# A two-block transformer step with 64 experts on one core: modulation's last sums taken in later, the transposed norm split between two engines, one head more between scores and transposes

## The chip, the cores and the metric

The kernel runs on one core of one Trainium2 chip. The metric is the device time of one execution in microseconds (us). Engines: PE (TensorE, matmuls; its weight loads are PEld), DVE (VectorE), ACT (ScalarE), POOL (GpSimd) and SP (SyncE, which issues nearly all loads). Each engine works through its own list of instructions in order; they meet at semaphores. Nothing is scheduled by hardware across engines, so the order in which the program issues work is the order in which an engine does it.

## What is computed

256 tokens of width 1024 go through two blocks. The first has a gated spatial branch and differential attention, ends in a layer norm, and shares the input projections. The second takes its scales, shifts and gates from a condition vector `c` (modulation), has two attentions (one with forget gates) and a mixture of 64 experts of which each token uses 6. All in fp32.

```python
def second_block(x, c, ...):
    cond = jax.nn.silu(c)
    for l in range(DEPTH):                                  # DEPTH is 1
        mod = cond @ w_mod[l] + b_mod[l]                    # 1024 x 6144
        shift_m, scale_m, gate_m, shift_f, scale_f, gate_f = ...split(mod, N_MOD)
        h = rms_norm_2(x, g_mix_norm[l]) * (1.0 + scale_m) + shift_m
        x = x + gate_m * hybrid_mixer(h, ...)
        h = rms_norm_2(x, g_ffn_norm[l]) * (1.0 + scale_f) + shift_f
        x = x + gate_f * moe_ffn(h, ...)
    return rms_norm_2(x, g_final)

# in hybrid_mixer
log_f = jax.nn.log_sigmoid((f_logit + b_forget).astype(jnp.float32))
cum_log_f = jnp.cumsum(log_f, axis=1).transpose(0, 2, 1)
o_fox = causal_block_attention(heads(fq), heads(fk), heads(fv), ..., cum_log_f)

# in the first block
lam = exp(sum(b_lam_q1 * b_lam_k1)) - exp(sum(b_lam_q2 * b_lam_k2)) + lam_init
x = layer_norm(DEEPNORM_ALPHA * x + mix_out + ple, ln_g[i], ln_b[i])
```

## The kernel before

**Dense stages (0 to about 600 us).** A matmul in fp32 is done as three: the weight is split into a rounded part (`hi`) and the rest (`lo`), the activations likewise, and hi by hi, lo by hi and hi by lo are summed. Weights come in slabs of 1 MB through SP's queue into 22 slots of 8 KB per partition. ACT casts a 512-column piece to `hi` (line 209), DVE subtracts it to give `lo` (line 210). `unit` (line 244 issues its matmuls where tokens are the moving side, line 242 the other way) runs one slab against 128 or 256 tokens, and calls `beat` after each group of three matmuls. `beat` is what orders the program: it advances the generators registered as streams (`yield n` means "go on n beats later"), then splits one more piece of a coming slab, or does one "extra", which is one sum of the modulation. `finish` runs a generator to its end at once. While `hold` is set, no extras are taken. Matmuls accumulate in three to five PSUM banks; the others (`bank()`) are handed out in turn.

**Early.** `early` makes the rope tables and SiLU of `c` with ACT's Sigmoid (line 765) and a POOL product; `prep_lam` (line 800) makes lambda with ACT's Exp (line 805). Each function needs a table of its own, loaded by an ACT_TABLE_LOAD. The rope of the first projections is DVE's `m` (lines 725 to 727), which reads an accumulation bank and so frees it.

**Modulation.** `w_mod` comes in 24 slabs, 8 for each of three blocks of two vectors. DVE adds each slab's products into `mod_acc` (line 580). `mod_finish` sums the 128 partitions by matmuls with ones (line 523), copies the sums (ACT, line 525), writes them to DRAM as `mod_line` (line 527, ACT's DMA queue), reads them back spread over partitions (line 538 for columns, 512 KB at line 535 for a gate), and adds the bias (DVE, lines 547 and 544). `mod_ready(blk)` forces the outstanding sums and then finishes the block's generator at once. For the last block that happens just ahead of the stage that multiplies by `w_out` (line 1395); `scale_f` (line 1414) follows.

**Norms.** `enter2(t)` does, for one half of the tokens, the layer norm that ends block 1, the rms norm `xn` (line 1119) and `scaled_T`: 8 transposes on PE (line 341), four to a bank, scaled and shifted by ACT into `hi` (lines 350, 354) and again by DVE into `val` (lines 352, 356), from which DVE subtracts `hi` (line 357).

**Attention of block 2.** `forget` makes `logf` on DVE and ACT (lines 1222 to 1229) and cumulates it with small matmuls (lines 1232 to 1234); DVE writes the result into a column of `lat_fq` and `fk` (lines 1237, 1238), which `heads_T` transposes (line 1274). `soft_heads` runs 16 heads in all, three steps of a head spread by `skewed`: `scores` (line 1284 on PE, maxima on DVE, Exp on ACT, division on DVE, line 1297), `transposed` (line 1305), `weighted` (line 1316):

```python
return b.skewed(range(8), (scores, transposed, weighted), 1)
```

While step i of the loop issues the scores of head i, it issues the transposes of head i-1 and the products of head i-2.

**Experts (about 612 to 1051 us).** 192 MB of expert weights come through SP. The first six experts' loads are issued as soon as slots are free, the others after the routing is known.

Of the kernel before, what the change touches and what calls it, by code (L numbers as in the profile page):

```python
# [68 lines left out]
class Builder:  # L69
# [54 lines left out]
    def tmp(self, shape, dtype, tag):  # L124
        size = 1
        for n in shape[1:]:
            size *= n
        kind, bufs = ("tiny", 12) if size <= 16 else ("small", 6) if size <= 64 else ("medium", 3) if size <= 128 else ("large", 4) if size <= 512 else ("huge", 2)
        if self.fixed:
            kind, bufs = tag, self.fixed.get(tag, 2)  # L130
        return self.work.tile(shape, dtype, tag=kind, name=self.name(tag), bufs=bufs)
# [124 lines left out]
    def beat(self):  # L256
# [11 lines left out]
        if self.quiet:  # L268
            return
        if self.hold or not (self.extras and (self.beats % 3 == 0 or not self.pieces) and self.extras[0][0](self.extras[0][1])):  # L270
# [26 lines left out]
    def skewed(items, stages, gap):  # L297

        n = len(items)
        for i in range(n + len(stages) - 1):  # L300
            for s, stage in enumerate(stages):
                if 0 <= i - s < n:
                    stage(items[i - s])
                yield gap
# [29 lines left out]
    def scaled_T(self, src, t, hi, lo, kts, scale, shift=None):  # L334

        nc = self.nc
        for k in range(0, kts, 4):
# [4 lines left out]
            val = self.tmp([P, n, P], F32, "val")  # L342
            h = hi[:, k:k + n, t * P:(t + 1) * P]
            l = lo[:, k:k + n, t * P:(t + 1) * P]
            for on_act in (True, False):
                for j in range(n):
                    i = ps[:, j * P:(j + 1) * P]
                    sc = scale[:, k + j:k + j + 1]
                    if shift is None and on_act:
                        nc.scalar.activation(h[:, j], i, AF.Copy, scale=sc)  # L350
                    elif shift is None:
                        nc.vector.tensor_scalar(val[:, j], i, sc, None, op0=OP.mult)
                    elif on_act:
                        nc.scalar.activation(h[:, j], i, AF.Identity, scale=sc, bias=shift[:, k + j:k + j + 1])
                    else:
                        nc.vector.tensor_scalar(val[:, j], i, sc, shift[:, k + j:k + j + 1], op0=OP.mult, op1=OP.add)
            nc.vector.tensor_tensor(l, val, h.bitcast(F32), op=OP.subtract)
            yield
# [3 lines left out]
def tile_block(ctx: ExitStack, tc: tile.TileContext, a: dict, out: bass.AP, taps=None):  # L362
# [154 lines left out]
    def mod_finish(blk):  # L517
# [10 lines left out]
        yield 8  # L528
# [10 lines left out]
        yield 8  # L539
# [13 lines left out]
    def mod_ready(blk):  # L553
        while len(mod_streams) <= blk:
            b.run_extra()
        for m in mod_streams[:blk + 1]:
# [203 lines left out]
    b.stream(rest_of_x(), 1)  # L760
    def early():
        tables(pos_i, freq, cos_t, sin_t)
        yield 14
        c_sig = b.tmp([P, KT], F32, "c_sig")
        nc.scalar.activation(c_sig, c_col, AF.Sigmoid)
        nc.gpsimd.tensor_tensor(c_col, c_col, c_sig, op=OP.mult)
# [30 lines left out]

    neg_lam = b.dense([P, 1], F32, "neg_lam")

    def prep_lam():  # L800
        pr = b.tmp([P, 2, 64], F32, "lam_pr")
        nc.vector.tensor_tensor(pr, lam_in[:, 0::2], lam_in[:, 1::2], op=OP.mult)
        sm = b.tmp([P, 2], F32, "lam_sm")
        nc.vector.tensor_reduce(sm, pr, axis=AX.X, op=OP.add)
        nc.scalar.activation(sm, sm, AF.Exp)
        nc.vector.tensor_tensor(neg_lam, sm[:, 1:2], sm[:, 0:1], op=OP.subtract)
        nc.vector.tensor_scalar(neg_lam, neg_lam, -LAM_INIT, None, op0=OP.add)
        yield

    s_lam = b.stream(prep_lam(), 20)  # L810
# [34 lines left out]
    b.finish(s_lam)  # L845
# [373 lines left out]
    def forget():  # L1219
# [10 lines left out]
        yield 6  # L1230
# [17 lines left out]
    g_fk.run((1,))  # L1248
    b.finish(s_lat)
# [28 lines left out]
    def soft_heads(qT, kT, width, v, which):  # L1278
# [43 lines left out]
        return b.skewed(range(8), (scores, transposed, weighted), 1)  # L1322
# [19 lines left out]
    g_fv.run()  # L1342
# [52 lines left out]
    mod_ready(2)  # L1395
# [587 lines left out]
```

## Time and profile before

| what | value |
|---|---|
| time, three runs | 1067.29, 1070.34, 1070.19 us; median 1070.19 |
| the profiled execution | 1065.67 us, of which the span from first to last instruction is 1064.0 |
| mean granted clock of TensorE | 0.963 |
| busy: PE, DVE, ACT, POOL | 968.5 (91%), 562.7 (53%), 412.0 (39%), 28.1 us (3%) |
| moved by DMA | 320.61 MB, 301 GB/s over the span |
| chain that ended last | PE 49%, DMA 32%, DVE 12%, ACT 3% |

How the rows further down are read. A row of the waits: the engine, tile and line that waited, "<-" and whom for, us in total, how often, the longest. A row of the timeline: start in us, length in us, engine, line, operation, output tile "<-" input tiles, shapes, how many in a row ("x4"), and in brackets the idle time of the engine just before it with what ended it. A row of the windows: the stretch in us and its length, then for PE, PEld, DVE, ACT and POOL the busy us and the number of instructions, then TensorE's granted clock as a share of full speed (1.00 is 2.4 GHz, 0.50 is 1.2 GHz), the share of the 16 DMA engines' time that was busy, and GB/s.

### The profile page before, as it was taken

Reading aid. Unit: us, or ns where it says so; the run is one execution under the profiler, and the core shown is the slowest. Engines: PE = TensorE matmul, PEld = TensorE weight load, DVE = VectorE, ACT = ScalarE, POOL = GpSimd, SP = SyncE. Lnnn points to the kernel's source line nnn. Section 1 sums busy time; section 2 is a strip of 40 time slices with the busy share of each in tenths; the row PEclk is TensorE's granted clock in tenths of the full one; section 3 lists DMA queues with packets and bytes.
Section 4 is the critical chain, followed back from the end, with each engine's and each line's share of the span. In section 5 each row is a group of like instructions: output and inputs, shape, how many; then the busy total and the mean of one; then the engine's idle time right before and its main releaser. Section 6 shows DMA issues by size and latency. Waiting matters only on the chain.

```text
span 1064.0 us, 17522 instructions
## 1 busy us (share of the span) xinstructions
PE 968.5 (91%) x6844; PEld 729.7 (69%) x6844; DVE 562.7 (53%) x1204; ACT 412.0 (39%) x897; POOL 28.1 (3%) x89
## 2 busy tenths in 40 slices
PE   8899999999998789898969989999978997699786
PEld 7789889899976677797947656766635664356432
DVE  6886777798879764757747433123322321022112
ACT  5565666554454454454624232121211221122102
POOL 0000000100000010000000100000000000000000
PEclk9999999999999898999989999999989998899988
DMA  8976249485984253253975799999999999999995
GB/s 270 334 268 230 98 144 339 142 307 205 367 290 158 79 206 121 80 198 127 376 319 197 299 417 384 421 422 421 420 420 421 420 421 420 421 420 421 421 415 212
DMA packets 83455, 320.61 MB, mean 301 GB/s; under 512 B 10013, under 2 KB 12317, under 8 KB 56362
## 3 DMA queue, kind: packets, MB, share of 16 engines
q1 hardware_dynamic: 82482, 318.37, 76.9%
q8 instruction: 55, 0.90, 0.3%
q10 hardware_dynamic: 888, 1.09, 0.3%
q14 instruction: 30, 0.25, 0.1%
HBM read 318.37 MB, written 1.07 MB: 300 GB/s over the span
## 4 chain that ended last, share of the span: by engine, by line
PE 49%; DMA 32%; DVE 12%; ACT 3%; issue 2%; SPq 0%; POOL 0%; ACTq 0%; DVEq 0%; POOLq 0%
PE bank L242 15%; PE bank L244 14%; DMA eu<-in_w_exp_up_dram 12%; DMA ed<-in_w_exp_down_dram 8%; DMA eg<-in_w_exp_gate_dram 7%; PE bank L1811 6%; DVE lo L210 5%; PE bank L1720 3%; PE bank L1664 2%; PE bank L1739 2%; DVE mod_acc L580 1%; DMA raw<-in_w_in_dram 1%; DMA mod_acc<-mod_line 1%; PE bank L1536 1%; PE bank L1274 1%
## 5 line engine op out<-in xcount | busy, mean ns | idle before, releaser
L210 DVE TENSOR_TENSOR lo<-raw,hi 128x512 fp32r<-128x512 f32 (+2 forms) x306 | 198.5, 687 | 50.3 <-ACT hi L209 49.5
L209 ACT CAST hi<-raw 128x512 fp32r<-128x512 f32 (+2 forms) x306 | 171.2, 620 | 53.6 <-DVE lo L210 25.8
L1811 PE MATMUL bank<-eu,xg 128*32 128x256 f32 (+1 forms) x1024 | 104.2, 416 | 21.6 <-DMA eu<-in_w_exp_up_dram 21.6
L1811 PE MATMUL bank<-eg,xg 128*32 128x256 f32 (+1 forms) x1024 | 104.5, 416 | 18.1 <-DMA eg<-in_w_exp_gate_dram 18.0
L1811 PEld LDWEIGHTS bank<-eg,xg 128*32 128x32 f32 (+1 forms) x1024 | 56.6, 133 | 71.1 <-DMA eg<-in_w_exp_gate_dram 25.5
L1817 DVE TENSOR_TENSOR hid<-bank,hid 128x256 f32<-128x256 f32 x24 | 10.2, 424 | 178.4 <-ACT hid L1816 178.4
L1811 PEld LDWEIGHTS bank<-eu,xg 128*32 128x32 f32 (+1 forms) x1024 | 58.0, 132 | 61.8 <-DMA eu<-in_w_exp_up_dram 28.9
L1720 PE MATMUL bank<-ed,hidT 128*64 128x512 f32 (+1 forms) x512 | 90.3, 597 | 1.1 <-ACT hidT L1712 0.6
L1816 ACT ACTIVATE hid<-bank 128x256 f32<-128x256 f32 x24 | 9.2, 384 | 191.8 <-PE bank L1811 191.8
L244 PE MATMUL bank<-hi,xTh 128*128 128x512 f32 x192 | 79.0, 412 | 4.3 <-DVE m L727 3.5
L244 PE MATMUL bank<-hi,xTl 128*128 128x512 f32 x192 | 75.7, 394 | 0.0
L244 PE MATMUL bank<-lo,xTh 128*128 128x512 f32 x192 | 74.8, 394 | 0.0
L242 PE MATMUL bank<-xTh,hi 128*128 128x256 f32 x256 | 73.6, 288 | 0.0
L242 PE MATMUL bank<-xTh,lo 128*128 128x256 f32 x256 | 72.4, 283 | 0.0
L242 PE MATMUL bank<-xTl,hi 128*128 128x256 f32 x256 | 72.4, 283 | 0.0
L1722 DVE SCALAR_TENSOR_TENSOR bank<-bank,gcol,gate_f 128x512 f32<-128x512 f32 x47 | 35.4, 754 | 53.7 <-PE bank L1720 53.7
L580 DVE SCALAR_TENSOR_TENSOR mod_acc<-wm,c_col,mod_acc 128x512 f32<-128x512 f32 x84 | 61.9, 744 | 0.0
L1668 ACT ACTIVATE xg<-bank,mod_col,scale_f 128x256 f32<-128x256 f32 x88 | 44.9, 561 | 41.6 <-PE bank L1664 41.6
L1720 PEld LDWEIGHTS bank<-ed,hidT 128*64 128x64 f32 (+1 forms) x512 | 26.9, 123 | 46.3 <-issue 37.1
L1728 ACT CAST y_hi<-bank 128x512 fp32r<-128x512 f32 x47 | 27.5, 585 | 78.3 <-DVE bank L1722 78.3
L1664 PE MATMUL bank<-S,xh_hi 128*128 128x256 f32 x176 | 49.2, 312 | 1.6 <-DVE y_lo L1729 1.3
L1729 DVE TENSOR_TENSOR y_lo<-bank,y_hi 128x512 fp32r<-128x512 f32 x47 | 32.5, 691 | 33.1 <-ACT y_hi L1728 33.1
(453 smaller groups left out, 1958.3 us busy)
## 6 DMA issues: line engine op xcount, KB each, us to landing
eg<-in_w_exp_gate_dram SPq DMA_DIRECT2D x64, 1024.0 KB, 19.7
eu<-in_w_exp_up_dram SPq DMA_DIRECT2D x60, 1024.0 KB, 19.7
ed<-in_w_exp_down_dram SPq DMA_DIRECT2D x60, 1024.0 KB, 19.8
raw<-in_w_in_dram SPq DMA_DIRECT2D x44, 1024.0 KB, 7.2
wm<-in_w_mod_dram SPq DMA_DIRECT2D x24, 1024.0 KB, 5.8
raw<-in_w_out_dram SPq DMA_DIRECT2D x8, 1024.0 KB, 9.9
raw<-in_w_in_dram SPq DMA_DIRECT2D x24, 256.0 KB, 4.8
raw<-in_w_branch_b_dram SPq DMA_DIRECT2D x4, 1024.0 KB, 5.2
```

The lines of the kernel that those rows point to most:

```text
L209: nc.scalar.copy(slab.hi[:, k], slab.raw[:, k])
L210: nc.vector.tensor_tensor(slab.lo[:, k], slab.raw[:, k], slab.hi[:, k].bitcast(F32), op=OP.subtract)
L242: nc.tensor.matmul(ps, w[:, k, c0:c0 + n], act[a][:, k0 + k], start=(k0 == 0 and i == 0), stop=stop, skip_group_check=True)
L244: nc.tensor.matmul(ps, act[a][:, k0 + k, t * P:(t + 1) * P], w[:, k, c0:c0 + n], start=(k0 == 0 and left[o] == 3 * slab.kts - 1), stop=stop)
L580: nc.vector.scalar_tensor_tensor(d, r, c_col[:, k:k + 1], d, op0=OP.mult, op1=OP.add)
L1664: nc.tensor.matmul(ps[:, 256 * j:256 * j + 256], part[:, t, k + j], S[q][:, t], start=(j == 0 and n == 0), stop=(n == 3), skip_group_check ...
L1668: nc.scalar.activation(xg[q][:, k + j], ps[:, 256 * j:256 * j + 256], AF.Identity, scale=scale_f[:, k + j:k + j + 1], bias=shift_f[:, k + ...
L1720: nc.tensor.matmul(ps[r], hid[p][:, k, r], experts[r0 + e, "d"][:, k, c * 512:(c + 1) * 512], start=(k == 0), stop=(k == 1))
L1722: nc.vector.scalar_tensor_tensor(yv, ps, gcol[p], gate_f[:, c * 512:(c + 1) * 512], op0=OP.mult, op1=OP.mult)
L1728: nc.scalar.copy(y_hi, yv)
L1729: nc.vector.tensor_tensor(y_lo, yv, y_hi.bitcast(F32), op=OP.subtract)
L1811: nc.tensor.matmul(ps[r, 256 * c:256 * c + 256], xg[q][:, k, c0 + cap * e:c0 + cap * (e + 1)], experts[r0 + e, what][:, k], start=(k == 0 ...
```

## The change

Seven edits:

1. `early` computes SiLU with Exp, together with lambda's Exp, so that one table load serves both; the sums of lambda come 10 beats in, the rest (five one- to eight-column DVE operations) later. `prep_lam` goes.
2. `scaled_T` issues all 8 transposes, then ACT scales the first bank and DVE the second into `val`, then ACT casts both to `hi` and DVE subtracts. While `hold` is set, every fourth beat splits no piece.
3. In `forget`, the pause before the cumulative sums is 9 beats instead of 6, and the forgetting attention's value projection (`g_fv`) has its first two units issued before those streams are finished.
4. `soft_heads` has an empty step between `scores` and `transposed`; the ring of tiles of up to 512 columns has 7 places instead of 4.
5. `mod_finish` waits 12 beats instead of 8 ahead of its reads, and 16 instead of 8 ahead of the last block's adds.
6. `mod_ready(2)` ahead of the `w_out` stage becomes `mod_summed(2)`, which forces the sums alone.
7. `mod_ready(2)` and `scale_f` stand inside the `w_out` stage, just ahead of the `split_lo` calls.

```diff
-"large", 4) if size <= 512
+"large", 7) if size <= 512
...
+        if self.hold and self.beats % 4 == 0:
+            return
...
+                if stage is None:
+                    continue
...
+                parts.append((k, n, ps, self.tmp([P, n, P], F32, "val")))
+        for k, n, ps, val in parts:
+            for j in range(n):
+                i = ps[:, j * P:(j + 1) * P]
+                sc = scale[:, k + j:k + j + 1]
+                if k and shift is None:
+                    nc.vector.tensor_scalar(val[:, j], i, sc, None, op0=OP.mult)
+                elif k:
+                    nc.vector.tensor_scalar(val[:, j], i, sc, shift[:, k + j:k + j + 1], op0=OP.mult, op1=OP.add)
...
+        for k, n, ps, val in parts:
             h = hi[:, k:k + n, t * P:(t + 1) * P]
...
+            nc.scalar.copy(h, val)
+            nc.vector.tensor_tensor(lo[:, k:k + n, t * P:(t + 1) * P], val, h.bitcast(F32), op=OP.subtract)
+        yield
...
         nc.scalar.dma_start(line, rows[0::32])
-        yield 8
+        yield 12
...
-        yield 8
+        yield (8, 8, 16)[blk]
...
+        yield 10
+        pr = b.tmp([P, 2, 64], F32, "lam_pr")
...
+        yield 5
+
+        nc.scalar.activation(sm[:, 2:], c_col, AF.Exp, scale=-1.0)
+        nc.scalar.activation(sm[:, :2], sm[:, :2], AF.Exp)
+        yield 5
...
+        nc.vector.tensor_scalar(sm[:, 2:], sm[:, 2:], 1.0, None, op0=OP.add)
+        nc.vector.reciprocal(sm[:, 2:], sm[:, 2:])
+        nc.vector.tensor_tensor(c_col, c_col, sm[:, 2:], op=OP.mult)
...
-        yield 6
+        yield 9
         ps = b.bank()
         nc.tensor.matmul(ps[:, 0:8], upper, logf[:, 0], start=True, stop=True)
...
     g_fk.run((1,))
+    for t in range(2):
+        g_fv.unit(0, t)
     b.finish(s_lat)
...
-        return b.skewed(range(8), (scores, transposed, weighted), 1)
+        return b.skewed(range(8), (scores, None, transposed, weighted), 1)
...
-    g_fv.run()
+    for t in range(2):
+        g_fv.unit(1, t)
...
-    mod_ready(2)
+    mod_ready(1)
+    mod_summed(2)
...
     gw2[0].unit(1, 1)
+    mod_ready(2)
+    nc.vector.scalar_tensor_tensor(scale_f, mod_col[:, 3], 1.0, g_ffn, op0=OP.add, op1=OP.mult)
     split_lo(0, 0)
```

How it moves instructions, at three places.

DVE around the last block's modulation, before (`m2Tl` is the last work ahead of the `w_out` stage, `lo` the pieces of that stage's slabs, `gm` and `base` its results, `xh` the norm ahead of the experts):

```order
L1019 TENSOR_TENSOR m2Tl_5492<-Ga_5093,m2Th_5490 128x512
L547 TENSOR_TENSOR mod_col<-mod_acc_3399,mod_col 128x8
L544 TENSOR_TENSOR gate_f<-mod_acc_3399,gate_f 128x1024
L1414 SCALAR_TENSOR_TENSOR scale_f<-mod_col,g_ffn 128x8
L210 TENSOR_TENSOR lo_5650<-raw_5422,hi_5649 128x512 x4
L210 TENSOR_TENSOR lo_5688<-raw_5440,hi_5687 128x512 x4
L1403 TENSOR_TENSOR gm_5720<-bank_768_5633,shelf_94 128x512
L1404 TENSOR_TENSOR base_3354<-gm_5720,base_3354 128x512
```

And with the change:

```order
L1026 TENSOR_TENSOR m2Tl_5478<-Ga_4980,m2Th_5476 128x512
L210 TENSOR_TENSOR lo_5622<-raw_5424,hi_5621 128x512 x4
L210 TENSOR_TENSOR lo_5668<-raw_5434,hi_5667 128x512 x4
L1414 TENSOR_TENSOR gm_5702<-bank_766_5607,shelf_94 128x512
...
L1437 TENSOR_SCALAR xh_5705<-base_3355,rms_rs_5723 128x1024
L1414 TENSOR_TENSOR gm_5757<-bank_775_5648,shelf_94 128x512
L1415 TENSOR_TENSOR base_3355<-gm_5757,base_3355 128x512
L553 TENSOR_TENSOR mod_col<-mod_acc_3400,mod_col 128x8
L550 TENSOR_TENSOR gate_f<-mod_acc_3400,gate_f 128x1024
L1560 SCALAR_TENSOR_TENSOR scale_f<-mod_col,g_ffn 128x8
L1540 TENSOR_TENSOR xh_lo_5764<-xh_5705,xh_hi_5742 128x64x8 x2
```

The three operations that need the reads have moved behind eight `lo` pieces, three pairs of `gm` and `base` and the first norm.

DVE around `logf`, before:

```order
L1229 TENSOR_TENSOR logf<-z_4089,ze_4094 128x16
L1237 TENSOR_SCALAR lat_fq_3746<-bank_531_4099 128x8
L1238 TENSOR_SCALAR fk_3748<-bank_531_4099 128x8
L210 TENSOR_TENSOR hi_lo_4119<-raw_4034,hi_lo_4119 128x1024
L580 SCALAR_TENSOR_TENSOR mod_acc_3399<-wm_4036,c_col,mod_acc_3399 128x512 x3
```

And with the change:

```order
L1236 TENSOR_TENSOR logf<-z_4076,ze_4081 128x16
L210 TENSOR_TENSOR hi_lo_4090<-raw_4022,hi_lo_4090 128x1024
L589 SCALAR_TENSOR_TENSOR mod_acc_3400<-wm_4024,c_col,mod_acc_3400 128x512 x3
L1244 TENSOR_SCALAR lat_fq_3737<-bank_535_4122 128x8
L1245 TENSOR_SCALAR fk_3739<-bank_535_4122 128x8
```

On PE 24 more matmuls stand ahead of the cumulative sums; on DVE a `lo` and three sums have come between `logf` and the columns that the head transposes read.

DVE from tile 0's scaled transposes to tile 1's statistics, before:

```order
L210 TENSOR_TENSOR lo_3670<-raw_3572,hi_3669 128x512
L356 TENSOR_SCALAR val_3684<-bank_463_3679,scale_m,mod_col 128x128 x4
L357 TENSOR_TENSOR hTl_3686<-val_3684,hTh_3685 128x4x128
L356 TENSOR_SCALAR val_3707<-bank_467_3702,scale_m,mod_col 128x128 x4
L357 TENSOR_TENSOR hTl_3686<-val_3707,hTh_3685 128x4x128
L1089 TENSOR_TENSOR base_3354<-bank_438_3520,base_3354 128x512
```

And with the change:

```order
L355 TENSOR_SCALAR val_3687<-bank_462_3682,scale_m,mod_col 128x128 x4
L363 TENSOR_TENSOR hTl_3698<-val_3681,hTh_3696 128x4x128
L363 TENSOR_TENSOR hTl_3698<-val_3687,hTh_3696 128x4x128
L210 TENSOR_TENSOR lo_3709<-raw_3573,hi_3708 128x512
L1096 TENSOR_TENSOR base_3355<-bank_437_3519,base_3355 128x512
```

One group of four copies is gone from DVE, and the piece stands behind the transposes' work instead of ahead of it. SP's loads keep their sequence throughout.

## Rows read from the trace of the kernel before

**Rows 1.** The page, part 1: busy us, share of the span, instructions.
```profile
PE 968.5 (91%) x6844; PEld 729.7 (69%) x6844; DVE 562.7 (53%) x1204; ACT 412.0 (39%) x897; POOL 28.1 (3%) x89
```

**Rows 2.** Windows by stage.
```profile
420.00:540.00 120.00, 109.53 (x847) 99.10 (x846) 88.32 (x206) 61.52 (x153) 0.64 (x7) 1.00 0.53 187
540.00:570.00 30.00, 19.76 (x76) 15.75 (x76) 13.44 (x24) 8.05 (x16) 0.38 (x1) 0.79 0.80 324
570.00:612.00 42.00, 40.95 (x301) 28.68 (x299) 23.64 (x92) 15.34 (x33) 4.21 (x8) 1.00 0.70 267
612.00:1051.00 439.00, 394.99 (x3184) 236.46 (x3184) 108.26 (x239) 92.03 (x187) 6.75 (x11) 0.96 1.01 415
```

**Rows 3.** PE's waits over the span: total us, times, longest.
```profile
PE bank L1811 <- DMA eu<-in_w_exp_up_dram: 21.6, 14, 2.4
...
PE bank L341 <- DVE xn L1119: 7.6, 2, 3.8
PE bank L1305 <- DVE pr L1297: 6.1, 6, 1.4
```

**Rows 4.** Windows behind PE's waits.
```profile
38.00:40.00 2.00, 2.00 (x6) 1.52 (x6) 2.00 (x5) 0.00 (x0) 0.00 (x0) 0.50 1.05 409
...
364.00:368.00 4.00, 4.00 (x14) 3.21 (x13) 2.06 (x5) 1.79 (x5) 0.00 (x0) 0.50 0.00 0
402.00:406.00 4.00, 4.00 (x15) 3.01 (x14) 0.95 (x1) 1.90 (x3) 0.00 (x0) 0.50 0.00 0
432.00:434.00 2.00, 2.00 (x16) 2.00 (x15) 2.00 (x6) 0.00 (x0) 0.00 (x0) 1.00 0.03 8
...
540.00:542.00 2.00, 2.00 (x6) 1.54 (x6) 1.23 (x3) 1.08 (x3) 0.00 (x0) 0.50 1.00 422
```

**Rows 5.** Timeline of ACT, DVE and PE, 31 to 38 us.
```profile
31.61 1.28 ACT L765 ACT_TABLE_LOAD   x1
...
33.66 2.61 DVE L210 TENSOR_TENSOR lo<-raw,hi 128x512 fp32r<-128x512 f32 x3 [1.34 <-ACT hi L209]
...
33.84 0.39 PE L244 MATMUL bank<-hi,xTh 128*128 128x512 f32 x1
34.07 0.39 PE L244 MATMUL bank<-lo,xTh 128*128 128x512 f32 x1
...
37.68 0.76 PE L244 MATMUL bank<-hi,xTh 128*128 128x512 f32 x1 [2.99 <-DVE m L727]
```

**Rows 6.** Timeline of DVE and PE, 349 to 372 us.
```profile
349.12 1.37 DVE L356 TENSOR_SCALAR val<-bank,scale_m,mod_col 128x128 f32<-128x128 f32 x4 [0.99 <-ACT hTh L354]
...
363.17 1.09 PE L341 MATMUL bank<-ident,xn 128*128 128x128 f32 x4 [3.84 <-DVE xn L1119]
...
372.00 0.80 PE L244 MATMUL bank<-lo,hTh 128*128 128x512 f32 x1 [1.23 <-DVE lo L210]
```

**Rows 7.** Timeline of PE and DVE, 399 to 408 us.
```profile
399.70 0.57 PE L1232 MATMUL bank<-logf,shelf 128*128 128x8 f32 x2 [4.33 <-DVE logf L1229]
...
405.05 1.23 DVE L210 TENSOR_TENSOR hi_lo<-raw,hi_lo 128x1024 fp32r<-128x1024 f32 x1 [3.50 <-ACT hi_lo L209]
406.20 2.07 DVE L580 SCALAR_TENSOR_TENSOR mod_acc<-wm,c_col,mod_acc 128x512 f32<-128x512 f32 x3
```

**Rows 8.** Timeline of PE at a head's scores.
```profile
430.63 0.68 PE L1284 MATMUL bank<-kT,qT 66*128 66x128 f32 x3 [1.68 <-DVE r L1192]
```

**Rows 9.** Timeline of PE and DVE, 537 to 560 us; the gate's read.
```profile
537.76 1.05 PE L523 MATMUL bank<-mod_acc,ones 128*32 128x512 f32 x2 [1.73 <-DVE mod_acc L580]
...
554.14 0.17 DVE L547 TENSOR_TENSOR mod_col<-mod_acc,mod_col 128x8 f32<-128x8 f32 x1 [8.56 <-DMA mod_acc<-mod_line]
558.01 1.23 DVE L544 TENSOR_TENSOR gate_f<-mod_acc,gate_f 128x1024 f32<-128x1024 f32 x1 [3.70 <-DMA mod_acc<-mod_line]
...
559.97 0.79 PE L244 MATMUL bank<-lo,m2Th 128*128 128x512 f32 x1 [10.24 <-DVE lo L210]
...
mod_acc<-mod_line ACTq DMA_DIRECT2D x1, 512.0 KB, 10.3
```

## What I expect, and why

> **What bounds the kernel now.** I read the page's busy shares first, then busy times by stage, then PE's waits, then the timeline around each wait. PE is busy 91% of the span [rows 1], so the time is PE's idle time plus PE's work at a lowered clock, stage by stage. By stage [rows 2]: from 612 to 1051 us the DMA share is 1.01 at 415 GB/s, so the expert stage ends when its bytes have come; PE's waits there are for expert slabs (21.6 us for "eu" alone [rows 3]). From 540 to 612 the DMA share is 0.80 and 0.70, so some 30 x 0.20 + 42 x 0.30 = 18.6 us of transfer time lie unused, because the loads wait for slots that the dense program frees. From 420 to 540 the share is 0.53. So the dense program sets when the expert loads run, and a microsecond saved before 600 should move the end by one microsecond. PE's waits there are for DVE: 7.6 us for "xn", 6.1 for "pr" [rows 3], 10.24 for one "lo" [rows 9].
>
> After the long waits the granted clock is 0.50, the lower level (1.2 GHz): 2 us at 38, 4 us at 364, 4 us at 402, 2 us at 540 [rows 4]. Work there takes twice as long, so half of each stretch is lost: 1, 2, 2 and 1 us. The clock stayed at 1.00 in 432 to 434 [rows 4], right behind a wait of 1.68 us [rows 8]; the rows show no loss behind a wait as short as that.
>
> **The change, part by part.**
>
> *Early tables.* Before, ACT loads a table for Sigmoid (31.61, 1.28 us) [rows 5]; DVE gets its next "hi" only then (1.34 us idle, 33.66), and PE waits 2.99 us until 37.68 for the "m" behind three "lo" (2.61 us) and the rope products. The change takes Exp for both, so one load fewer, and puts five small DVE operations behind that "m". DVE then has a "hi" whenever it wants one: "m" comes 1.34 us earlier by that wait, and earlier still because ACT's last cast of the slab and DVE's "lo" for it no longer stand behind lambda's sums and its Exp. No row shows that alone; it is worth between 0 and the rest of the wait, 1.65, and I take 1.25, as "m" then has nothing ahead of it but its own "lo". That makes 2.6 and leaves PE a wait of 0.4. With the 1 us of clock, and some of the slower work up to 38: **4 us** (bounds 2 and 4.5: the idle time less a new wait of 1, and all of both).
>
> The Trainium skill (ScalarE: Activation LUTs, What ACT_TABLE_LOAD costs) gives a switch as 1.28 us of load and 1.38 us of drain, 2.66 together. By it the load that stays would hold the casts 1.38 us longer, and the gain would be about 3.7, estimated from that page. The trace disagrees: DVE's "lo" starts at 33.66, 0.77 us after the load has ended [rows 5], and the Sigmoid and a cast lie in between.
>
> *Transposed norm.* Per token tile DVE drops one of two groups of four scaled copies (1.37 us) and the wait for ACT between them (0.99) [rows 6]; ACT exchanges four scaled copies for two casts. Also one "lo" goes from ahead of the copies to behind them and one from ahead of the statistics (0.6 each, half of the 1.23 that 1024 columns take [rows 7]). For tile 0 nothing shortens its own "xn". Tile 1's DVE chain from the end of tile 0's copies is then 1.37 + 0.99 + 0.6 = 3.0 us earlier, and its "xn" with it: of PE's 3.84 us at 363.17 some 0.6 to 0.8 stay. Behind it PE waits again for pieces that stand behind tile 1's copies (until 372.00 [rows 6]); there 1.37 goes again and the exchange with ACT once instead of twice. PE's clock loss, 2 us [rows 4], goes with the long wait. 3.1 + 2 + about 2 of the wait that ends at 372.00: **7 us** (bounds 3 and 8.5).
>
> *logf.* PE stands 4.33 us before the cumulative sums at 399.70 [rows 7]. In the order, eight beats of 3 matmuls come ahead of them now, 24 at 0.23 us (two such at full clock start 0.23 apart [rows 5]), 5.5 us of work that has to be done anyway. So this wait ends. But DVE now has a "lo" (1.23) and three sums (2.07) [rows 7] between logf and the columns that PE's head transposes read: 3.3 us, of which PE covers the rest with 0.6 of sums and 0.7 of one beat; a new wait of some 1.8 us follows. 4.33 + 2 of clock - 1.8 + 1 of the beats that ran slow ahead of 402: **5.5 us** (bounds 3, if the new wait lowers the clock too, and 7).
>
> *A head more between scores and transposes.* PE's waits for "pr" are 6.1 us in 6 of the 16 heads, and 1.68 [rows 3, 8] for a rope product that DVE does too late. With one head more in between, "pr" is a head's beats older when it is transposed. DVE's queue stays as long, so some of it returns for a score bank or a rope product: **4.5 us** (bounds 1 and 7.5).
>
> *Modulation's last sums.* Today DVE is blocked from 545.6 to 558.0 by the two reads (8.56 + 3.70 idle [rows 9]), the next slab's "lo" is queued behind them, and PE waits 10.24 us. Ahead of that PE waited 1.73 at 537.76 for the last sum, with 1 us of clock behind it [rows 4]; behind 559.97 I take 1.5 more, between the 1 and the 2 shown after other waits. Gross 1.73 + 10.24 + 2.5 = 14.5. Added: the sums' copy and write stand between the next slab's first and second cast, about 1 us of PE wait. The adds (1.23 for the gate [rows 9] and 0.3) now lie on DVE's way to the routing: 1.5. The reads start later too: on the old clock the write goes out some 3 us later, behind a cast, so the gate's line lands at 561 instead of 558.0; PE, from 538 on, needs 7 units of 12 matmuls, 19.3 us, and the 1 above, and DVE two operations more, so DVE comes to the adds at about 560: 1. **11 us** (bounds 8 and 13). SP's loads keep their sequence; one load loses its slot and comes with the next group, into transfer time that is free.
>
> The gate's 512 KB landed 10.3 us after their issue, among expert loads of 1024 KB [rows 9]. The Trainium skill (DMA: Bandwidth & Descriptors, Queues, rings and completion order) says that each DMA engine takes turns between queues packet by packet, so a read on ACT's queue should not stand behind all of SP's. By an even share the read would take about 2.5 us, an estimate from that page and 415 GB/s; then DVE would not wait and the sum be 1 larger. The 10.3 us do not bear that out.
>
> **Sum.** 4 + 7 + 5.5 + 4.5 + 11 = 32. The profiled execution took 1065.67 us (span 1064.0), 4.5 under the median of 1070.19; against the median, 1070.2 - 32 = **1038 us**. All lower bounds give 2 + 3 + 3 + 1 + 8 = 17, or 1053; all upper 40.5, or 1029.7.
>
> **Rivals.**
> 1. *The waits come back on DVE.* DVE is 88.3 us busy in the 120 of 420 to 540 [rows 2], and every part but the third only reorders its queue. Then each part gives its lower bound: 1053. For: three of the five waits name DVE. Against: in the first, third and fifth the wait is for another engine or a DMA that DVE itself waits for, and this is what is moved.
> 2. *The transfers cap it.* If the loads before 612 cannot come earlier, only the unused 18.6 us can be won, less the 2 or 3 that short gaps keep: 1070 - 16 = 1054. Against: the share of 0.53 before 540.
> 3. *Slower: the attention loses its clock.* The changed step order makes each head's transposes wait for a bank held by the head before, and the waits grow past 1.68 us, where the clock held, to the 1.73 of 537.76, where it fell. A head then costs 1.73 + 1 of clock, and if the low clock lasts as at 402 to 406, 1.73 + 2 = 3.7. All 16 heads: 60, less the 27.5 of the other parts: 1070 + 32 = 1102. It decides from nine heads on (9 x 3.7 = 33 against 27.5 + 3.2). For: so small a margin. Against: DVE is at 74% there and has the head's "pr" ready earlier than today.
> 4. *It does not do what it says:* the reads at the end land so late that DVE holds the routing as long as it held PE. With the gate at 572 instead of 561 the fifth part gives nothing: 1070 - 21 = 1049. Against: a read of 10.3 us would have to take twice that.
>
> **How the numbers follow.** Forecast, 1030 to 1046: 0.62. Rival 1: 0.20. Rival 2: 0.06. Rival 4: 0.06. Rival 3: 0.03. No net effect, several small ones cancelling: 0.03. A measurement of this kernel tells about 0.3%, 3.2 us, from no change. Faster by more: 0.62 + 0.20 + 0.06 + 0.06 = 0.94, less a little for their own tails, 0.92. Same 0.04, slower 0.04. The range runs from all upper bounds to just past rival 2: 1029 to 1055.
>
> **What would show it.** Right: no wait of PE over 1 us for "m"; none over 1 us for "xn" on tile 1, while tile 0's 3.8 us stays; no wait at the cumulative sums, a new one near 1.8 us for "lat_fq" just behind; waits for "pr" under 2 us in all; PE busy through the former 549 to 560, DVE's wait for the reads under 2 us; expert stage as long as before, starting 32 us earlier. Wrong: an expert stage that starts early but ends late (rival 2), PE waits of the same total under other names (1), a granted clock under 0.9 in the attention (3), or a DVE wait for "mod_acc" over 8 us ahead of the routing (4).

## The result: 26 us faster, and the profile after

With the change one execution takes 1042.34 us (median of four, 1041.75 to 1043.60) against 1068.98 for the kernel before, beside which it ran: a ratio of 0.9753 [0.9733, 0.9773], or 26.4 us at 1069. (Below, kernels are compared by their ratios to the kernel before, times 1069; the difference of two such ratios is uncertain by some 2.8 us, from their two intervals.) The forecast was 1038 in 1029 to 1055. The profiled execution took 1042.16 us, its span 1040.5.

The page of the kernel after, part 1 (answers to [rows 1]): PE does the same 6844 matmuls.

```profile
PE 962.2 (92%) x6844; PEld 721.2 (69%) x6844; DVE 559.1 (54%) x1193; ACT 411.1 (40%) x896; POOL 27.8 (3%) x88
```

Windows by stage of the kernel after (answer to [rows 2]; the expert stage now begins some 26 us earlier):

```profile
420.00:540.00 120.00, 113.70 (x828) 100.94 (x829) 90.05 (x199) 62.69 (x152) 0.64 (x7) 0.97 0.59 218
540.00:570.00 30.00, 29.05 (x183) 21.38 (x183) 23.18 (x85) 13.66 (x31) 2.43 (x3) 1.00 0.75 299
570.00:612.00 42.00, 39.28 (x294) 25.19 (x291) 13.98 (x38) 11.37 (x22) 2.70 (x6) 1.00 0.97 392
612.00:1030.00 418.00, 375.71 (x3039) 220.99 (x3038) 98.69 (x218) 83.89 (x170) 6.14 (x10) 0.96 0.99 410
```

From 540 to 570 PE was busy 19.76 us at a clock of 0.79; now it is 29.05 at 1.00. From 570 to 612 the DMA share has gone from 0.70 to 0.97 and the rate from 267 to 392 GB/s: the expert stage starts there, and its transfers run near the rate that they have behind 612 (415 GB/s before, 410 now).

PE's waits over the span (answer to [rows 3]):

```profile
PE bank L346 <- DVE xn L1126: 4.5, 2, 3.7
PE bank L1314 <- DVE r L1199: 3.7, 1, 3.7
...
PE bank L244 <- DVE m L736: 2.5, 3, 1.1
PE bank L1325 <- DVE aT L1316: 2.5, 3, 1.6
PE bank L244 <- DVE sga L1065: 2.2, 1, 2.2
```

The waits for "logf", "pr" and the long "lo" are gone, and of the two for "xn" one is left at full length; "m" has gone from 3.5 us in two waits to 2.5 in three; this "r", "aT" and "sga" are new. PE's timeline at the places of the five terms:

```profile
35.73 0.47 PE L244 MATMUL bank<-hi,xTh 128*128 128x512 f32 x1 [1.08 <-DVE m L736]
...
296.47 0.50 PE L244 MATMUL bank<-hi,xTh 128*128 128x512 f32 x1 [2.23 <-DVE sga L1065]
...
345.27 1.44 PE L346 MATMUL bank<-ident,xn 128*128 128x128 f32 x8 [3.67 <-DVE xn L1126]
361.69 1.13 PE L346 MATMUL bank<-ident,xn 128*128 128x128 f32 x8 [0.83 <-DVE xn L1126]
366.15 0.50 PE L244 MATMUL bank<-hi,hTh 128*128 128x512 f32 x1 [1.24 <-ACT hi L209]
...
394.71 0.28 PE L1239 MATMUL bank<-logf,shelf 128*128 128x8 f32 x2
...
397.26 0.60 PE L1283 MATMUL bank<-ident,lat_fq 128*66 128x128 f32 x4 [1.03 <-DVE lat_fq L1244]
...
423.07 0.87 PE L1314 MATMUL bank<-ident,pr 128*128 128x128 f32 x3 [3.66 <-DVE r L1199]
...
524.81 2.13 PE L529 MATMUL bank<-mod_acc,ones 128*32 128x512 f32 x8
...
537.35 0.50 PE L244 MATMUL bank<-lo,m2Th 128*128 128x512 f32 x1 [0.23 <-DVE lo L210]
```

And DVE's, where the tables and the modulation's reads are:

```profile
54.22 0.49 DVE L587 TENSOR_SCALAR mod_acc<-wm,c_col 128x512 f32<-128x512 f32 x1 [2.62 <-DMA wm<-in_w_mod_dram]
...
525.10 0.75 DVE L589 SCALAR_TENSOR_TENSOR mod_acc<-wm,c_col,mod_acc 128x512 f32<-128x512 f32 x1
...
546.95 0.16 DVE L553 TENSOR_TENSOR mod_col<-mod_acc,mod_col 128x8 f32<-128x8 f32 x1
547.03 1.22 DVE L550 TENSOR_TENSOR gate_f<-mod_acc,gate_f 128x1024 f32<-128x1024 f32 x1
```

To see where time was won, lay the two traces side by side: take an instruction that both have, with the same matmuls ahead of it on PE, and subtract its starts. The difference is how far the kernel after is ahead at that place.

| instruction (start before, after) | ahead by | what was won or lost since the row above |
|---|---|---|
| transposes of `ws_m` (44.01, 40.61) | 3.4 | early tables: 3.4 |
| unit at 63.36, 61.07 | 2.3 | lost 1.1, behind DVE's wait for `wm` |
| unit at 233.50, 232.96 | 0.5 | lost 1.8, most of it at 231, behind the first block's modulation |
| around 320 | -1.6 | lost 2.1, most of it the "sga" wait |
| around 375, behind the norm | 6.5 | 8.1 |
| cumulative sums to 413, less 24 moved matmuls | 12 | 5.5 to 6 |
| products of `om` (532.61, 520.33) | 12.3 | heads: 0.3 |
| in the first `w_out` unit (542.45, 526.87), behind the sums | 15.6 | last sum and its clock: 3.3 |
| the unit behind the long "lo" (563.07, 535.80) | 27.3 | reads: 11.7 |
| the norm ahead of the experts (580.79, 554.31) | 26.5 | -0.8 |

The 4.1 us that an expectation below goes by is the start of the transposes of `p`, 49.70 before and 45.64 after; on PE they stand one group of three matmuls (0.7 us) further ahead now, so 3.4 of the 4.1 are gain.

Behind that the expert stage kept most of it: the spans differ by 1064.0 - 1040.5 = 23.5 in the profiled executions, of which the one before was 3.3 under its median here. So 3.0 of the 26.5 were not kept in this pair. The same shows in the undoings below: ahead of the experts they are 8.3 (norm), 8.8 (logf), 4.7 (heads) and 9.5 (modulation) behind the kernel after, at the end 6.7, 7.0, 3.7 and 7.1.

### The profile page after: what moved, and what is told of

The parts are those of the page before. It is cut to its first block, busy times and chain, and to the rows that moved or that the text cites. A ratio compares the mean times of both kernels' runs of the same rounds, so it can differ in the third digit from the quotient of the medians.

```text
span 1040.5 us, 17503 instructions
## 1 busy us (share of the span) xinstructions
PE 962.2 (92%) x6844; PEld 721.2 (69%) x6844; DVE 559.1 (54%) x1193; ACT 411.1 (40%) x896; POOL 27.8 (3%) x88
## 4 chain that ended last, share of the span: by engine, by line
PE 30%; DMA 22%; DVE 12%; ACT 5%; issue 1%; POOL 0%; ACTq 0%; DVEq 0%; SPq 0%; POOLq 0%
DMA eu<-in_w_exp_up_dram 11%; PE bank L1823 9%; DMA ed<-in_w_exp_down_dram 7%; PE bank L1732 5%; DVE lo L210 4%; PE bank L244 4%; DMA eg<-in_w_exp_gate_dram 4%; PE bank L1676 3%; PE bank L1751 3%; PE bank L242 2%; DVE mod_acc L589 1%; PE bank L1465 1%; ACT hi L209 1%; PE bank L1283 1%; ACT pr L1303 1%
## 5 line engine op out<-in xcount | busy, mean ns | idle before, releaser
L1732 PEld LDWEIGHTS bank<-ed,hidT 128*64 128x64 f32 (+1 forms) x512 | 26.4, 123 | 48.6 <-issue 37.5
```

The costliest lines, as they stand in the source:

```text
L1732: nc.tensor.matmul(ps[r], hid[p][:, k, r], experts[r0 + e, "d"][:, k, c * 512:(c + 1) * 512], start=(k == 0), stop=(k == 1))
```

## The experiments

**Each part undone alone.** Five kernels, each the kernel after with one part as it was. If the terms add up, each gives back its own.

*The early tables* (edit 1): Sigmoid and `prep_lam` back.

```diff
-        yield 10
-        pr = b.tmp([P, 2, 64], F32, "lam_pr")
...
+        yield 14
+        c_sig = b.tmp([P, KT], F32, "c_sig")
+        nc.scalar.activation(c_sig, c_col, AF.Sigmoid)
+        nc.gpsimd.tensor_tensor(c_col, c_col, c_sig, op=OP.mult)
...
+    s_lam = b.stream(prep_lam(), 20)
```

> The changed kernel with edit 1 undone (Sigmoid table, lambda as before). Theory A: PE's 4.1 us won at 50 us are given back by 61 us because DVE then waits 2.6 us for a modulation slab whose transfer cannot come sooner (DMA at full rate since 36 us); undone, 0 to 2 us slower than 1042.3 (1042 to 1044.5), and the 2.6 us DVE wait for wm is gone. Theory B: the gain is real to the end and what is lost between 50 and 330 us comes from another edit; undone 1046.

1042.06 us, 0.9763 [0.9746, 0.9780]: 1.1 slower than the change by the ratios, not told from nothing. PE's wait is back, and DVE's for `wm` is gone. PE's timeline, then DVE's, of this kernel:

```profile
37.62 0.47 PE L244 MATMUL bank<-hi,xTh 128*128 128x512 f32 x1 [3.00 <-DVE m L736]
```

```profile
56.00 0.87 DVE L587 TENSOR_SCALAR mod_acc<-wm,c_col 128x512 f32<-128x512 f32 x2
```

DVE comes to the first sum at 56.00 with no wait in the bracket; in the kernel after it stood there from 51.6 to 54.22. PE is 1.9 behind the kernel after from 38 to 55 us, and 0.7 from 62 us on. So 1.2 of the 1.9 us is won and given back within 25 us, because the transfers there are already at their rate. The other 1.5 of the 3.4 in the table is clock: behind the wait of 2.99 us the kernel before ran at 0.50 [rows 4], and behind its 3.00 us this one ran at 1.00 (last section). The DMA view of the kernel after, 36 to 62 us:

```profile
GB/s 248 334 397 406 413 406 406 391 388 381 391 388 381 391 388 381 391 394 375 397 419 429 429 429 328 416 381 384 429 429 413 435 366 400 372 384 284 110 72 16
...
wm<-in_w_mod_dram SPq DMA_DIRECT2D x2, 1024.0 KB, 12.1
```

*The transposed norm* (edit 2): both engines on each bank again, no skipped beat.

```diff
-        if self.hold and self.beats % 4 == 0:
-            return
...
+            for on_act in (True, False):
...
+            nc.vector.tensor_tensor(l, val, h.bitcast(F32), op=OP.subtract)
+            yield
```

> The changed kernel with edit 2 undone (each engine its own half of every bank, no skipped beat under hold). Theory A: the shift between the traces grows by 8.1 us from 348 to 375 us, all of it this edit's; undone 1050, tile 1's wait for xn back at 3 to 4 us. Theory B: part of those 8 us is only the pieces put off by the skipped beats and comes back elsewhere; undone 1046 or less.

1049.72 us, 0.9843 [0.9825, 0.9861]: 9.6 slower. PE's timeline of this kernel shows tile 1's wait back at full length, and the two behind it:

```profile
365.18 1.09 PE L343 MATMUL bank<-ident,xn 128*128 128x128 f32 x4 [3.77 <-DVE xn L1122]
...
372.27 0.49 PE L244 MATMUL bank<-hi,hTh 128*128 128x512 f32 x1 [1.42 <-ACT hi L209]
...
374.01 0.79 PE L244 MATMUL bank<-lo,hTh 128*128 128x512 f32 x1 [1.24 <-DVE lo L210]
```

From 414 us to the experts it is 8.3 behind.

*logf* (edit 3): pause 6, `g_fv` in one piece.

```diff
-        yield 9
+        yield 6
...
-    for t in range(2):
-        g_fv.unit(0, t)
...
-    for t in range(2):
-        g_fv.unit(1, t)
+    g_fv.run()
```

> The changed kernel with edit 3 undone (pause of 6 beats, the value projection after the streams). Theory A, from the two traces side by side: the edit wins 6 us between 389 and 407 us (the wait of 4.3, its clock, less a new wait of 1.0); undone 1048, with the wait at the cumulative sums back at about 4 us. Theory B: undone, the first head's scores come earlier against the gate products and the waits for r and aT in the attention shrink, so only half comes back: 1045.

1049.06 us, 0.9822 [0.9802, 0.9842]: 7.4 slower. PE's timeline:

```profile
393.28 0.36 PE L1239 MATMUL bank<-logf,shelf 128*128 128x8 f32 x2 [3.78 <-DVE logf L1236]
...
535.84 1.04 PE L529 MATMUL bank<-mod_acc,ones 128*32 128x512 f32 x2 [2.07 <-DVE mod_acc L589]
```

The first row is the wait that the edit removes. The second was not expected to be its doing: the wait for the modulation's last sum, as before the change [rows 9].

*A head more* (edit 4): the empty step out, 4 places in the ring.

```diff
-"large", 7) if size <= 512
+"large", 4) if size <= 512
...
-        return b.skewed(range(8), (scores, None, transposed, weighted), 1)
+        return b.skewed(range(8), (scores, transposed, weighted), 1)
```

> The changed kernel with edit 4 undone (scores and transposes a head apart as before, ring of 4). Theory A, from PE's order laid side by side: between the scores of the first head and the second attention's output the two kernels keep the same distance, so the edit only trades PE's waits for pr (6.1 us) and r (1.7) for waits for r at a bank (3.7), for aT (2.5) and a lowered clock; undone, the time stays within 2 us of the changed kernel's 1042.3 (1041 to 1044.5) and the waits for pr are back. Theory B, the prediction's: the edit is worth 4.5, so 1047.

1045.58 us, 0.9794 [0.9778, 0.9811]: 4.4 slower, the size that was forecast, but not where. Its waits for "pr" are 3.5 us again, while "r" costs 3.0 instead of 3.7; laid beside the kernel after, the first products of `of` stand 2.2 behind and those of `om` 1.2, about the 1.8 with which it came to the heads. (Those 1.8 are no part of the heads: the wait for "sga" at 297, first row below, 2.31 here and 2.23 in the kernel after, was followed by a lowered clock here and not there.) In PE's timeline:

```profile
296.99 0.62 PE L244 MATMUL bank<-hi,xTh 128*128 128x512 f32 x1 [2.31 <-DVE sga L1065]
...
528.70 1.06 PE L529 MATMUL bank<-mod_acc,ones 128*32 128x512 f32 x6
531.83 1.05 PE L529 MATMUL bank<-mod_acc,ones 128*32 128x512 f32 x2 [2.07 <-DVE mod_acc L589]
```

and its window there:

```profile
530.00:535.00 5.00, 3.17 (x7) 1.95 (x8) 4.19 (x7) 2.09 (x5) 0.00 (x0) 0.77 0.59 200
```

From 1.2 behind at 524 us it comes out 4.7 behind at 542, so 3.5 is lost here. DVE's timeline says why:

```profile
526.41 0.74 DVE L589 SCALAR_TENSOR_TENSOR mod_acc<-wm,c_col,mod_acc 128x512 f32<-128x512 f32 x1
...
531.03 0.74 DVE L589 SCALAR_TENSOR_TENSOR mod_acc<-wm,c_col,mod_acc 128x512 f32<-128x512 f32 x1
```

In the kernel after the last sum (525.10) stands where this kernel has its last but one (526.41). The one sum that is left over lies 4.6 us later, behind `Ga`, `m2Tl` and two more `lo` in DVE's queue, and PE waits for it. Edits 3 and 4 each have to be there for the sum to come in time; undo either and the same wait of 2.07 us returns. (With edits 5 to 7 undone, below, 0.82 of it is there.) The payoff of 3.5 to 4 us is one, and shows in both undoings.

*Modulation* (edits 5 to 7): pauses 8, `mod_ready(2)` and `scale_f` ahead of the stage.

```diff
-        yield 12
+        yield 8
...
-        yield (8, 8, 16)[blk]
+        yield 8
...
-    mod_ready(1)
-    mod_summed(2)
+    mod_ready(2)
...
+    nc.vector.scalar_tensor_tensor(scale_f, mod_col[:, 3], 1.0, g_ffn, op0=OP.add, op1=OP.mult)
...
-    mod_ready(2)
-    nc.vector.scalar_tensor_tensor(scale_f, mod_col[:, 3], 1.0, g_ffn, op0=OP.add, op1=OP.mult)
```

> The changed kernel with edits 5, 6 and 7 undone (the last block's modulation finished at once ahead of the output projection). Theory A: 14.2 us of shift between 520 and 565 us, of which the expert stage keeps back about 3 because it then starts with fewer slabs on hand; undone 1053 to 1056, PE's wait for lo back at about 10 us. Theory B: the longer pauses of edit 5 cost time for the first two blocks (a slot given back later, loads later at 203 and 262 us); then undoing also wins 2 to 3 us back: 1050 to 1053, with DVE earlier at 210 us.

1050.15 us, 0.9838 [0.9820, 0.9856]: 9.1 slower. DVE's timeline, then PE's:

```profile
539.54 0.17 DVE L553 TENSOR_TENSOR mod_col<-mod_acc,mod_col 128x8 f32<-128x8 f32 x1 [9.92 <-DMA mod_acc<-mod_line]
```

```profile
535.83 0.50 PE L244 MATMUL bank<-hi,m2Th 128*128 128x512 f32 x1 [3.36 <-ACT hi L209]
...
542.58 0.80 PE L244 MATMUL bank<-lo,m2Th 128*128 128x512 f32 x1 [6.25 <-DVE lo L210]
```

DVE again stands before the reads, and PE behind ACT and DVE, 9.6 us in two waits. But from 296 to 510 us this kernel is about 3 *ahead* of the kernel after: something in the modulation edits costs time much earlier. Three more kernels look for it.

**Modulation taken apart.** The kernel before with edits 6 and 7 and the last block's pauses alone:

```diff
-        yield 8
+        yield (8, 8, 12)[blk]
...
-        yield 8
+        yield (8, 8, 16)[blk]
...
-    mod_ready(2)
+    mod_ready(1)
+    mod_summed(2)
...
```

> The kernel before with edits 6 and 7 and the last block's pauses alone (first two blocks unchanged). Theory A: the terms add up, so this part alone is worth the 12 to 14 us that it moves between 520 and 565 us: 1055 to 1056 against 1068. Theory B: the part depends on the others (the shorter head distance leaves the last sums late, so PE still waits for mod_acc, and DVE waits for the reads): 8 to 10 us, 1058 to 1060.

1054.61 us, 0.9873 [0.9853, 0.9893]: 13.6 faster than before, by itself. It is 2.1 behind the kernel before at the last sum, 0.5 behind at 544 and 11.5 ahead at 564. The reads are worth the 12 from 544 on; the 1.6 ahead of that is clock, 1.00 here from 540 to 543 and 0.50 before [rows 4]. The last sum is not theirs; PE's timeline:

```profile
539.83 1.04 PE L523 MATMUL bank<-mod_acc,ones 128*32 128x512 f32 x2 [1.73 <-DVE mod_acc L583]
```

And the kernel after, with 8 beats again ahead of the first two blocks' reads:

```diff
-        yield 12
+        yield (8, 8, 12)[blk]
```

> The changed kernel with edit 5 kept for the last block alone: the pause ahead of the reads is 8 beats again for the first two blocks. Theory B of the last runs, now A: the longer pause keeps the first block's accumulator in its slot about 2 us longer, loads at 203 and 262 us come later and DVE waits for them; with 8 beats tile 0's xn comes 3 us earlier and the time is 1039 (ratio to before 0.972 to 0.973). Theory B: what cost 3 us was not the pause but the order of DVE and ACT work around it, which the last-block edits also change; then 1042 as the changed kernel.

1037.87 us (five runs, 1037.77 to 1038.65), 0.9723 [0.9707, 0.9740]: 3.2 faster than the change by the ratios, at the edge of what they tell, and 4.5 by the spans (1036.0). Its median is the lowest here. PE is 0.9 ahead at 61 us, where the programs do not differ yet; 2.6 at 240, 4.9 at 300, 3.8 ahead of the experts. The waits at 231 and for "sga" are gone. They stand in all five kernels with 12 beats (the one after and the undoings of edits 1 to 4), and neither in the kernel before nor with the modulation edits undone. At 200 us one sees how the first of them arises. SP's waits from 196 to 216 us:

```profile
SPq L182 <- DVE mod_col L553: 0.3, 1, 0.3
```

and SP's and ACT's timelines:

```profile
200.30 0.37 SPq L182 DMA_DIRECT2D raw<-in_w_in_dram  x1
```

```profile
206.98 1.14 ACT L209 CAST hi<-raw 128x512 fp32r<-128x512 f32 x2 [3.78 <-DMA raw<-in_w_in_dram]
```

In the kernel after the same two, from SP's and ACT's timelines:

```profile
202.23 0.37 SPq L182 DMA_DIRECT2D raw<-in_w_in_dram  x1
```

```profile
208.91 1.14 ACT L209 CAST hi<-raw 128x512 fp32r<-128x512 f32 x2 [4.85 <-DMA raw<-in_w_in_dram]
```

`mod_finish` holds the slot of `mod_acc` until its adds are done (DVE's `mod_col`). With 8 beats that slot is the next load's: SP waits 0.3 for `mod_col` and issues at 200.30. With 12 beats that load waits for another slab's `lo` instead, since `mod_col` comes later still (202.78). It goes out 1.9 later, of which 0.9 is the lag from 61 us (SP's load ahead of it stands at 199.51 and 200.37); the other 1.1 is the longer wait of ACT for that slab, 4.85 instead of 3.78.

**Longer, shorter.** If a held slot is what costs, holding a slab longer must cost more, and less may win. Each from the kernel just described: the sums 18 beats after their load's issue instead of 10; 8 instead of 10; and 6 instead of 8 in both of the first two blocks' pauses.

```diff
-            if "raw" not in box or not force and b.beats - box["at"] < 10:
+            if "raw" not in box or not force and b.beats - box["at"] < 18:
```

> As the last, and a modulation sum waits for 18 beats after its slab's load instead of 10. Theory A: DVE's 2.6 us wait for the first slab at 54 us goes, PE's wait for m at 61 us too, and half of the early gain stays: 1 to 2 us under the run with 8 beats (1037 to 1038). Theory B: DVE reaches the same transfers later anyway (they go at full rate from 36 to 59 us), or sums put off pile up ahead of the output projection: same as it, or 1 to 3 slower.

1059.95 us, 0.9932 [0.9916, 0.9948]: 22 slower, far more than either theory had. DVE's wait for `wm` is gone, and with it the loss at 61 us: PE is 3.1 ahead of the kernel before at 57 us and still at 88. But it is 4.6 behind the kernel with 10 beats at 223 us, 8.8 at 304, 11.4 at 350, 14 at 511, and 21 behind the last sums. The waits on PE:

```profile
PE bank L242 <- DVE lo L210: 5.6, 5, 2.6
...
PE bank L529 <- DVE mod_acc L589: 4.0, 2, 2.3
PE bank L242 <- ACT hi L209: 3.7, 2, 2.7
```

"lo" and "hi" are the pieces of slabs that come later; that they do because 24 `wm` slabs each keep their slot longer fits the places, but was not traced load by load. The last 7 of the 21 arise at the sums themselves: they were put off up to the place that needs them, and PE waits 1.68 and 2.32 us for them.

> As the run with 8 beats, but a modulation sum waits for 8 beats after its load instead of 10; at 18 it cost 22 us. Theory A: what cost 22 us was slots held longer by slabs that had landed, so 8 frees them sooner and wins 1 to 3 us (1035 to 1037). Theory B: at 8 DVE reaches slabs that haven't landed and waits, in order, for them: DVE waits for wm of 2 us and more, and 1039 to 1042.

1041.37 us, 0.9748 [0.9724, 0.9773].

> As the run with 8 beats, but 6 beats at both pauses for the first two blocks. Theory A: every beat by which the accumulator's slot comes back earlier brings loads forward; 1 to 2 us under 1037.9. Theory B: at 8 the slot is no longer what the loads wait for, and at 6 ACT and DVE wait for the reads themselves: 1037 to 1040.

1039.73 us, 0.9736 [0.9711, 0.9761]. Neither is told from the 0.9723 of 10 and 8 beats; neither wins.

**Two terms measured again** from the faster kernel, since the lowered clock at 297 had come into the undoing of the heads.

> The run with 8 beats, with edit 1 undone. Beside the longer pauses the edit was worth 1 us. Theory A: transfers at full rate up to 59 us cap it whatever comes later, 1 to 2 us: 1039 to 1040. Theory B: the pauses had hidden its worth (DVE waited for loads anyway), and now it shows 3 to 4: 1041 to 1042.

1039.75 us, 0.9738 [0.9709, 0.9766]: 1.6 for the early tables, again not told from nothing.

> The run with 8 beats, with edit 4 undone. Undone beside the longer pauses, it cost 4 us, none of it at the heads: 1.8 from a lowered clock at 298 us, the rest because the last sums came later and PE waited 2.1 us for them with a lowered clock behind. Theory A: the late sums belong to the edit, the clock at 298 was chance: 1040 to 1041, with PE's wait for mod_acc at 2 us. Theory B: both were chance: 1038.

1041.54 us, 0.9752 [0.9725, 0.9780]: 3.1 for the heads, by itself within what the ratios leave open (3.4). The clock at 298 is 1.00 here. It is 2.2 behind at 85 us, where the programs do not differ yet, 2.3 at the products of `om`, and 5.8 behind the last sum, for which PE waits 2.06. So the last sum costs 3.5 again, and the heads nothing that shows.

## Why the prediction was right, and which terms were off

The direction and the place of the gain were right, and the total fell within the range, 26.4 us against a forecast of 32, all of it ahead of 600 us. By place, the 26.5 us ahead of the experts are 2.3 from the early tables, 8.1 from the norm, 5.5 from logf, 0.3 from the heads, 3.3 from the last sum and 10.9 from the reads, less 3.9 at 231 and 297. That they add up so near to the forecast is in part luck, as the terms show:

- **Early tables: forecast 4, kept about 1.** The local gain was 3.4: 1.9 of PE's wait, which went from 2.99 to 1.08 and not to 0.4 (so the sign "no wait over 1 us" just failed), and 1.5 of clock, which came with the one trace [rows 4] and is in neither undoing. The 1.25 that the prediction took beside the 1.34 of DVE's wait was twice too large. The 3.7 that it estimated from the Trainium skill (ScalarE: Activation LUTs, What ACT_TABLE_LOAD costs) stands nearer to 3.4 than its 4 does, but not for the drain by which it was worked out: none shows behind the load that stays. ACT's timeline of the kernel after:

```profile
29.22 1.28 ACT L781 ACT_TABLE_LOAD   x1
30.51 0.21 ACT L781 ACTIVATE lam_sm<-c_col 128x8 f32<-128x8 f32 x1
```

  What failed besides is the step that took a local gain as kept: "a microsecond saved before 600 should move the end by one". At 51.60 DVE came to `wm` ahead of its transfer, with the DMA engines at a share of 0.96 from 36 to 62 us, and everything behind it in DVE's order waited 2.62. That is rival 2, in one stage of the five, where the prediction did not look for it.
- **Transposed norm: forecast 7, measured 9.6 by the undoing and 8.1 in the traces.** Tile 1's wait is 0.83 (forecast 0.6 to 0.8), and tile 0's stays at 3.67. The two waits behind tile 1 were 1.48 and 1.23 us, and 1.24 and 0.22 are left, so the "about 2" of the prediction is 1.25. The clock gave back more than its 2: before, it was 0.50 from 364 to 368 us and again 0.59 from 372 to 376, after, 1.00 from 360 to 376. So 4.3 of the 8.1 are waits, and the rest is about what the clock gave back.
- **logf: forecast 5.5, measured 5.5 to 6 at the place and 7.4 by the undoing.** The wait for logf is gone; the one for "lat_fq" is 1.03 instead of 1.8. What the undoing shows beyond that is the last sum.
- **A head more: forecast 4.5, measured 4.4, for another reason.** "pr" went (6.1 before), but "r" (3.66 at once, with the clock at 0.50 behind it) and "aT" (2.5) came: 0.3 in the heads. So here rival 1 held, the waits came back on DVE. The payoff is the last sum (3.5), which was in no step of this term, with 1.8 of a clock that fell at 297. That the number fits is luck.
- **Modulation: forecast 11, measured 9.1; 12 at the place and 13.6 by the run for the reads alone, less some 3 to 4 for edit 5's pauses.** Errors that nearly cancel. The 1.73 for the last sum, with its clock, was booked here but belongs to edits 3 and 4: the kernel with the modulation edits alone still has the wait. Without it the term had 10.24 + 1.5 of clock, less 3.5 for work and reads that DVE would meet later; of the 3.5 at most 0.8 came about (last row of the table). The reads landed in 7.7 and 6.5 us, DVE found them at 546.95 and 547.03 without idle time, and PE waited 0.23. On the other side the longer pause of the first two blocks was not priced at all. It holds a slot, and the slab that would have taken it came 1.1 us later for that. PE lost 1.8 at 231 and 2.1 around 297.

The five undoings add up to 1.1 + 9.6 + 7.4 + 4.4 + 9.1 = 31.6, 5.2 more than the change gave. Their uncertainties together could hide that; but one cause of overlap is shown, the last sum, which counts in two of them, and the 1.8 of clock in the undoing of the heads belong to no edit.

Rival 3 did not come, though a wait like the one that it feared did once: the transposes of `pr` wait for a bank, but for DVE's rope product "r" to free it and not for the head before. The windows of the kernel after, behind that wait:

```profile
423.00:425.00 2.00, 1.93 (x9) 1.96 (x10) 1.97 (x8) 0.00 (x0) 0.64 (x7) 0.50 0.00 0
425.00:427.00 2.00, 2.00 (x7) 1.61 (x6) 0.92 (x5) 1.73 (x6) 0.00 (x0) 0.50 0.03 8
```

One wait in 16 heads, where nine were needed; from 420 to 540 the clock is still 0.97. Rival 4 fell: no read was waited for.

Why DVE's place for the last sum depends on edits 3 and 4 was read from its order and times; a kernel that changes that place alone was not run. That the longer pause costs through the slot rests on the one load shown, on the two waits that every kernel with 12 beats has, and less surely on the kernel that holds slabs longer; the later stretch, where the lead grows from 2.6 to 4.9 at 240 to 300 us, was not traced load by load. Why part of what was saved ahead of the experts is not kept at the end stays open.

## What to carry to other kernels

In this kernel a wait that was removed early was kept only as far as the next stage's transfers came early too: look at the DMA rate right behind the place before booking the gain. Do not book the clock behind a wait from one trace: the same wait was followed by the lower clock in one trace and by the upper in another. Price a pause by what it holds (a slot, a bank) and by whom that keeps waiting, not by the beats themselves. When parts are undone one by one, look where the time comes back: here two parts own the same wait, and one of them paid off a hundred microseconds behind the place that it changes. When two traces are laid side by side, count the matmuls ahead of the instruction first, as an instruction that has moved by one group shows a gain that is none.

## What was not expected of the hardware

Waits of nearly the same length, at the same instruction, were followed by different clocks. For "m" at 38 us, 2.99 us were followed by 0.50 in the kernel before [rows 4, 5], and 3.00 us by 1.00 with the early tables undone. For the last sum, 1.73 us were followed by 0.50 before [rows 4, 9], and 1.73 us by 1.00 with the modulation edits alone. For "sga", 2.23 us were followed by 1.00 in the kernel after, and 2.31 us by 0.56 without the extra head. The windows right behind, each from a kernel of its own: early tables undone, modulation edits alone, after, extra head undone.

```profile
38.00:40.00 2.00, 2.00 (x10) 1.62 (x9) 2.00 (x5) 0.00 (x0) 0.00 (x0) 1.00 1.05 410
```

```profile
540.00:543.00 3.00, 3.00 (x15) 1.95 (x14) 2.87 (x5) 0.01 (x1) 0.00 (x0) 1.00 0.73 227
```

```profile
296.50:299.00 2.50, 2.50 (x11) 2.08 (x12) 1.81 (x3) 1.66 (x3) 0.00 (x0) 1.00 0.00 0
```

```profile
297.00:299.00 2.00, 2.00 (x5) 1.61 (x6) 1.32 (x3) 1.30 (x3) 0.00 (x0) 0.56 0.00 0
```

The prediction's distinction between 1.68 us (kept) and 1.73 (lowered) [rows 4, 8, 9] was thus no boundary. What decides is not shown by these runs.
